# Bilinear form against 128 matrices: weights laid out in 64-row halves, in 19 transfers of uneven size

## The chip, the cores and the metric

One core of a Trainium2 chip. The metric is the device time of one execution in microseconds, the lower the better.

## The reference

For each row b of x and y, and each of 128 weight matrices, one number is computed:

```python
batch, dim_i, dim_j, dim_k = 32, 256, 256, 128
# x: (32, 256), y: (32, 256), weight: (128, 256, 256), all float32
out = np.einsum('bi,bj,kij->bk', x, y, weight)     # (32, 128)
```

The weight is 33.6 MB in fp32 and each of its elements is used for 32 rows of x. x, y and the output are small: 32 KB, 32 KB and 16 KB.

## The kernel before

The sum over i is done on TensorE, with 32 columns of x transposed as the stationary operand and the weight as the moving one; the sum over j, with y, is done on VectorE, which multiplies a row of results by y and adds it up.

At the start x and y come in over the SyncE queue (L51, L54). An identity matrix is made on GpSimd, TensorE transposes x in two pieces (L62), and VectorE casts them to bf16 into `xT` (L67). The piece `ii` holds the rows i = 2p + ii of x on partition p.

The weight comes in 16 tiles of eight k each. A tile (`wtile`, bf16, 128 partitions x 8 x 512) is one transfer, issued by GpSimd (L77), which also casts fp32 to bf16 on the way. A partition p holds the rows 2p and 2p + 1 of each of the eight matrices: 512 consecutive elements, 2 KB of fp32, for each k. There are four buffers, so GpSimd issues the first four transfers at once and then each next one when TensorE has finished with the tile four places ahead.

For each two k of a tile, two matmuls of 512 columns (two k by 256 j) add up the even and the odd rows in one PSUM tile (L82). For each single k VectorE then makes one multiply and add over 256 elements (L93), which leaves one column of `out_sb`. A second short VectorE instruction reads the accumulator out. At the end SyncE stores `out_sb` (L104).

Each engine works through its list in the order in which the loops below are written; the tile framework adds the semaphore waits.

Of the kernel before, what the change touches and what calls it, by code (L numbers as in the profile page):

```python
# [1 line left out]

# [5 lines left out]


@with_exitstack
def kernel(
    ctx: ExitStack,
    tc: tile.TileContext,
    x: bass.AP,
    y: bass.AP,
    weight: bass.AP,
    out: bass.AP,
):
    nc = tc.nc  # L20
    P = 128

    B, I = x.shape
    _, J = y.shape
    K, _, _ = weight.shape
    assert x.shape == (B, I)
    assert y.shape == (B, J)
    assert weight.shape == (K, I, J)
    assert out.shape == (B, K)

    assert I % P == 0
    I_TILES = I // P
    assert K <= P

    K_TILE = 8
    assert K % K_TILE == 0
    NUM_K_TILES = K // K_TILE
    K_SUB = max(1, 512 // J)
    assert K_TILE % K_SUB == 0

    f32 = mybir.dt.float32
    bf16 = mybir.dt.bfloat16

    consts = ctx.enter_context(tc.tile_pool(name="consts", bufs=1))
    wpool = ctx.enter_context(tc.tile_pool(name="wpool", bufs=4))
    psum_pool = ctx.enter_context(tc.tile_pool(name="psum", bufs=6, space=bass.MemoryType.PSUM))
    tpsum_pool = ctx.enter_context(tc.tile_pool(name="tpsum", bufs=2, space=bass.MemoryType.PSUM))
    tmps = ctx.enter_context(tc.tile_pool(name="tmps", bufs=4))

    x_sb = consts.tile([B, I], f32)  # L50
    nc.sync.dma_start(out=x_sb, in_=x)  # L51

    y_sb = consts.tile([B, J], f32)
    nc.sync.dma_start(out=y_sb, in_=y)  # L54

    identB = consts.tile([B, B], f32)
    make_identity(nc, identB)

    xT = consts.tile([P, I_TILES, B], bf16)
    for ii in range(I_TILES):  # L60
        xt_psum = tpsum_pool.tile([P, B], f32)
        nc.tensor.transpose(  # L62
            out=xt_psum,
            in_=x_sb[:, ii::I_TILES],
            identity=identB,
        )
        nc.vector.tensor_copy(out=xT[:, ii, :], in_=xt_psum)  # L67

    out_sb = consts.tile([B, K], f32)

    w_rearr = weight.rearrange("k (i ii) j -> i k (ii j)", ii=I_TILES)

    for kt in range(NUM_K_TILES):
        k0 = kt * K_TILE

        wtile = wpool.tile([P, K_TILE, I_TILES * J], bf16)
        nc.gpsimd.dma_start(out=wtile, in_=w_rearr[:, k0:k0 + K_TILE, :])  # L77

        for ks in range(0, K_TILE, K_SUB):
            psum = psum_pool.tile([P, K_SUB * J], f32)  # L80
            for ii in range(I_TILES):
                nc.tensor.matmul(  # L82
                    out=psum[:B, :].rearrange("b (k j) -> b k j", k=K_SUB),
                    lhsT=xT[:, ii, :],
                    rhs=wtile[:, ks:ks + K_SUB, ii * J:(ii + 1) * J],
                    start=(ii == 0),
                    stop=(ii == I_TILES - 1),
                )

            psum_view = psum[:B, :].rearrange("b (k j) -> b k j", k=K_SUB)  # L90
            for kk in range(K_SUB):
                tmp = tmps.tile([B, J], f32)
                nc.vector.tensor_tensor_reduce(  # L93
                    out=tmp,
                    in0=psum_view[:, kk, :],
                    in1=y_sb,
                    scale=1.0,
                    scalar=0.0,
                    op0=mybir.AluOpType.mult,
                    op1=mybir.AluOpType.add,  # L100
                    accum_out=out_sb[:, k0 + ks + kk:k0 + ks + kk + 1],
                )

    nc.sync.dma_start(out=out, in_=out_sb)  # L104


# [1 line left out]
_INS = ['x', 'y', 'weight']  # L108
_OUTS = [((32, 128), 'float32')]


# [23 lines left out]
```

## Time and profile before

| | us |
|---|---|
| median of 4 runs | 96.57 |
| lowest and highest run | 95.49, 96.80 |
| the profiled execution | 96.36 |
| its span, first to last instruction | 94.5 |
| TensorE matmul busy | 48.3 (51%) |
| VectorE busy | 48.1 (51%) |
| GpSimd busy | 14.6 (15%) |

The time of an execution is a little longer than the span that the profile shows, here by 1.86 us. TensorE and VectorE are each busy for half of the span, and the profile's mean granted clock of TensorE is 0.756 of full speed. The granted clock has two levels, shown as 0.50 (1.2 GHz) and 1.00 (2.4 GHz). DMA rates are counted in bytes written, which for the weight are half of the bytes read.

### The profile page before, as it was taken

What the parts mean: (1) busy time and instruction counts of PE and PEld (TensorE: products, weight loads), DVE (VectorE), ACT (ScalarE), POOL (GpSimd) and SP (SyncE); (2) the same over time, 40 slices, a digit from 0 to 9 for tenths busy, and PEclk for the clock granted to TensorE, in tenths of its full rate; (3) what the DMA queues carried; (4) which work ended last, traced back from release to release, by engine and by line L of the source; (5) the groups of instructions that cost most, each with busy time, mean ns of one, the idle gap of its engine ahead of it and who ended that gap; (6) DMA issues with size and microseconds to landing.
All of it is one profiled execution on the core that took longest, in us unless ns stands there. A gap on an engine that the chain in (4) does not pass through costs nothing.

```text
span 94.5 us, 680 instructions
## 1 busy us (share of the span) xinstructions
PE 48.3 (51%) x130; PEld 15.0 (16%) x130; DVE 48.1 (51%) x258; POOL 14.6 (15%) x22
## 2 busy tenths in 40 slices
PE   0100096775248293937083773935092958761560
PEld 0100031212011130302030211211030303120210
DVE  0100048383919175667456281849275483948290
POOL 5910002012300303030303002032003000000000
PEclk9999999999995555579975555589955555599955
DMA  0699999999999999999999999999999999996000
GB/s 24 67 170 200 147 207 207 208 205 208 207 209 205 208 206 207 208 206 208 207 208 206 208 204 207 206 210 205 208 207 207 208 206 208 206 208 110 3 3 7
DMA packets 16787, 16.88 MB, mean 179 GB/s; under 512 B 304, under 2 KB 16784, under 8 KB 16784
## 3 DMA queue, kind: packets, MB, share of 16 engines
q0 software_dynamic: 16640, 16.78, 108.1%
q1 hardware_dynamic: 144, 0.08, 0.3%
q14 instruction: 3, 0.02, 0.1%
HBM read 33.62 MB, written 0.02 MB: 356 GB/s over the span
## 4 chain that ended last, share of the span: by engine, by line
DMA 78%; PE 9%; issue 6%; POOL 3%; DVE 1%; POOLq 0%; DVEq 0%
DMA wtile<-in_weight_dram 78%; PE psum L82 9%; POOL wtile L77 3%; DVE tmp L93 1%; POOL identB masks.py:199 0%; POOL identB masks.py:197 0%; POOLq masks.py:199 0%; POOLq L130 0%; POOLq L77 0%; POOLq L119 0%; DVE out_sb L93 0%; DVEq L130 0%
## 5 line engine op out<-in xcount | busy, mean ns | idle before, releaser
L82 PE MATMUL psum<-wtile,xT 128*32 128x512 bf16 x128 | 47.9, 541 | 40.4 <-DMA wtile<-in_weight_dram 40.4
L93 DVE CUSTOM_DVE_ANT_0 tmp<-psum,y_sb 32x256 f32<-32x256 f32 x128 | 47.3, 409 | 41.1 <-PE psum L82 38.5
L82 PEld LDWEIGHTS <-xT 128*32 128x32 bf16 x128 | 14.7, 122 | 72.8 <-issue 50.8
L77 POOL DMA_DIRECT2D wtile<-in_weight_dram x16 | 14.1, 886 | 57.6 <-PE psum L82 57.1
L93 DVE DVE_READ_ACCUMULATOR2_ANT out_sb<- 32x1 f32 x128 | 9.1, 71 | 0.0
L67 DVE CAST xT<-xt_psum 128x32 bf16<-128x32 f32 x2 | 0.3, 191 | 3.0 <-PE xt_psum L62 3.0
L62 PE MATMUL xt_psum<-identB,x_sb 32*128 32x32 f32 x2 | 0.4, 312 | 2.7 <-POOL identB masks.py:199 2.7
L62 PEld LDWEIGHTS xt_psum<-identB,x_sb 32*128 32x128 f32 x2 | 0.3, 201 | 2.7 <-POOL identB masks.py:199 2.7
masks.py:199 POOL TENSOR_SCALAR_AFFINE_SELECT identB<-identB 32x32 f32<-32x32 f32 x1 | 0.2, 224 | 0.1
masks.py:197 POOL MEMSET identB<- 32x32 f32 x1 | 0.1, 114 | 0.3 <-POOLq L119 0.3
L119 POOL MEMSET const-float32-0.0<- 128x1 f32 x1 | 0.1, 103 | 0.2 <-issue 0.2
L119 POOL MEMSET const-bfloat16-1.0<- 128x1 bf16 x1 | 0.1, 106 | 0.0
L119 POOL MEMSET const-uint8-127<- 128x1 uint8 x1 | 0.1, 106 | 0.0
L119 POOL MEMSET const-float32-1.0<- 128x1 f32 x1 | 0.1, 103 | 0.0
## 6 DMA issues: line engine op xcount, KB each, us to landing
wtile<-in_weight_dram POOLq DMA_DIRECT2D x16, 1024.0 KB, 16.7
x_sb<-in_x_dram SPq DMA_DIRECT2D x1, 32.0 KB, 1.7
y_sb<-in_y_dram SPq DMA_DIRECT2D x1, 32.0 KB, 1.7
out_dram<-out_sb SPq DMA_DIRECT2D x1, 16.0 KB, 1.4
```

What stands on the lines that cost most here:

```text
L62: nc.tensor.transpose(out=xt_psum, in_=x_sb[:, ii::I_TILES], identity=identB,)
L67: nc.vector.tensor_copy(out=xT[:, ii, :], in_=xt_psum)
L77: nc.gpsimd.dma_start(out=wtile, in_=w_rearr[:, k0:k0 + K_TILE, :])
L82: nc.tensor.matmul(out=psum[:B, :].rearrange("b (k j) -> b k j", k=K_SUB), lhsT=xT[:, ii, :], rhs=wtile[:, ks:ks + K_SUB, ii * J:(ii + 1) ...
L93: nc.vector.tensor_tensor_reduce(out=tmp, in0=psum_view[:, kk, :], in1=y_sb, scale=1.0, scalar=0.0, op0=mybir.AluOpType.mult, op1=mybir.Al ...
L119: nc = _bacc.Bacc("TRN2", target_bir_lowering=False, num_devices=1)
```

## The change

Four things change together.

**Layout of the weight.** A partition now holds four consecutive rows of a matrix (4p to 4p + 3, 1,024 elements, 4 KB of fp32) instead of two. A matrix of 256 rows then fills 64 partitions, and two matrices stand one above the other: the even k of a pair on partitions 0 to 63 (`kg` = 0), the odd k on 64 to 127 (`kg` = 1). A full tile still holds eight k, as 128 x 4 x 1024.

**Matmuls.** For each pair of k there are four steps (`ic`), and in each a matmul of 64 rows and 256 columns for the even k on the upper half and one for the odd k on the lower half, into two PSUM tiles. That makes 512 matmuls of 256 columns in place of 128 of 512. `xT` holds four pieces instead of two, each twice, once per half of the partitions; for that x is loaded twice side by side (`x2_sb`) and four transposes and casts are made.

**Transfers.** The 16 transfers of eight k become 19: one of four k, 14 of eight, then 4, 4, 2 and 2.

**Buffers.** PSUM has four tiles of 256 columns for the results (six of 512 before), and the output scratch `tmp` two buffers instead of four.

```diff
-    K_TILE = 8
-    K_SUB = max(1, 512 // J)
+    CHUNK = 4
+    HALF_P = P // 2
+    K_TILE = 4
+    K_HALF = K_TILE // 2
+    K_SUB = max(1, min(K_HALF, 256 // J))
...
-    psum_pool = ctx.enter_context(tc.tile_pool(name="psum", bufs=6, space=bass.MemoryType.PSUM))
-    tpsum_pool = ctx.enter_context(tc.tile_pool(name="tpsum", bufs=2, space=bass.MemoryType.PSUM))
-    tmps = ctx.enter_context(tc.tile_pool(name="tmps", bufs=4))
+    psum_pool = ctx.enter_context(tc.tile_pool(name="psum", bufs=4, space=bass.MemoryType.PSUM))
+    tmps = ctx.enter_context(tc.tile_pool(name="tmps", bufs=2))
-    x_sb = consts.tile([B, I], f32)
-    nc.sync.dma_start(out=x_sb, in_=x)
+    x2_sb = consts.tile([B, 2, I], f32)
+    nc.sync.dma_start(out=x2_sb[:, 0, :], in_=x)
+    nc.sync.dma_start(out=x2_sb[:, 1, :], in_=x)
+    x2_flat = x2_sb.rearrange("b two i -> b (two i)")
...
-    xT = consts.tile([P, I_TILES, B], bf16)
-    for ii in range(I_TILES):
+    xT = consts.tile([P, CHUNK, B], bf16)
+    for ic in range(CHUNK):
...
-            in_=x_sb[:, ii::I_TILES],
+            in_=x2_flat[:, ic::CHUNK],
...
-    w_rearr = weight.rearrange("k (i ii) j -> i k (ii j)", ii=I_TILES)
-    for kt in range(NUM_K_TILES):
-        k0 = kt * K_TILE
-        wtile = wpool.tile([P, K_TILE, I_TILES * J], bf16)
-        nc.gpsimd.dma_start(out=wtile, in_=w_rearr[:, k0:k0 + K_TILE, :])
-        for ks in range(0, K_TILE, K_SUB):
-            psum = psum_pool.tile([P, K_SUB * J], f32)
-            for ii in range(I_TILES):
-                nc.tensor.matmul(
-                    out=psum[:B, :].rearrange("b (k j) -> b k j", k=K_SUB),
-                    lhsT=xT[:, ii, :],
-                    rhs=wtile[:, ks:ks + K_SUB, ii * J:(ii + 1) * J],
+    w_rearr = weight.rearrange(
+        "(k2 kg) (ip ic) j -> (kg ip) k2 (ic j)", kg=2, ic=CHUNK)
+    sizes = [4] + [8] * 14 + [4, 4, 2, 2]
+    k0 = 0
+    for size in sizes:
+        K_HALF = size // 2
+        wtile = wpool.tile([P, 4, CHUNK * J], bf16)
+        nc.gpsimd.dma_start(
+            out=wtile[:, :K_HALF, :],
+            in_=w_rearr[:, k0 // 2:k0 // 2 + K_HALF, :],
+        )
+        for ks in range(0, K_HALF, K_SUB):
+            psums = []
+            for kg in range(2):
+                psum = psum_pool.tile([P, K_SUB * J], f32)
+                psums.append(psum)
+            for ic in range(CHUNK):
+                for kg in range(2):
+                    p0 = kg * HALF_P
+                    nc.tensor.matmul(
+                        out=psums[kg][:B, :].rearrange(
+                            "b (k j) -> b k j", k=K_SUB
+                        ),
+                        lhsT=xT[p0:p0 + HALF_P, ic, :],
+                        rhs=wtile[p0:p0 + HALF_P, ks:ks + K_SUB,
+                                  ic * J:(ic + 1) * J],
+                        start=(ic == 0),
+                        stop=(ic == CHUNK - 1),
+                    )
...
+                    kdst = k0 + 2 * (ks + kk) + kg
...
-                    accum_out=out_sb[:, k0 + ks + kk:k0 + ks + kk + 1],
+                        accum_out=out_sb[:, kdst:kdst + 1],
```

The order on TensorE, before, around the step from the first weight tile to the second (`wtile_87` and `wtile_117`; numbers tell buffers apart, and what a row waits for stands in brackets):

```order
L82 LDWEIGHTS xT_79
L82 MATMUL psum_110<-wtile_87,xT_79 32x512
L82 LDWEIGHTS xT_79
L82 MATMUL psum_110<-wtile_87,xT_79 32x512
L82 LDWEIGHTS xT_79
L82 MATMUL psum_119<-wtile_117,xT_79 32x512 [waits DMASW1_49]
```

And on TensorE now, at the same step (`wtile_91` is the first tile, of four k, and `wtile_121` the second, of eight):

```order
L99 MATMUL psum_107<-wtile_91,xT_77 32x256
L99 LDWEIGHTS xT_77
L99 MATMUL psum_108<-wtile_91,xT_77 32x256
L99 LDWEIGHTS xT_77 [waits DMASW1_49]
L99 MATMUL psum_123<-wtile_121,xT_77 32x256 [waits DVE_49]
L99 LDWEIGHTS xT_77
L99 MATMUL psum_124<-wtile_121,xT_77 32x256 [waits DVE_49]
L99 LDWEIGHTS xT_77
L99 MATMUL psum_123<-wtile_121,xT_77 32x256
```

Two matmuls of one PSUM tile stood behind each other; now the matmuls of two PSUM tiles alternate, each with a weight load of its own ahead of it, and there are 32 pairs of load and matmul for a full tile in place of eight.

The last weight transfers in GpSimd's list, before:

```order
L77 DMA wtile_447<-in_weight_dram 128x8x512 [waits DMASW0_49,PE_49]
L77 DMA wtile_477<-in_weight_dram 128x8x512 [waits DMASW1_49,PE_49]
L77 DMA wtile_507<-in_weight_dram 128x8x512 [waits DMASW2_49,PE_49]
L77 DMA wtile_537<-in_weight_dram 128x8x512 [waits DMASW3_49,PE_49]
L130 UNCONDITIONAL_BRANCH
```

And now:

```order
L86 DMA wtile_817<-in_weight_dram 128x4x1024 [waits DMASW1_49,PE_49]
L86 DMA wtile_875<-in_weight_dram 128x4x1024 [waits DMASW2_49,PE_49]
L86 DMA wtile_933<-in_weight_dram 128x2x1024 [waits DMASW3_49,PE_49]
L86 DMA wtile_963<-in_weight_dram 128x2x1024 [waits DMASW4_49,PE_49]
L86 DMA wtile_993<-in_weight_dram 128x1024 [waits DMASW5_49,PE_49]
L86 DMA wtile_1009<-in_weight_dram 128x1024 [waits DMASW6_49,PE_49]
```

The last full transfer (`wtile_875`) has four smaller ones behind it, each of which still waits for TensorE (`PE_49`) to leave the buffer four places ahead; the last one takes over the buffer of `wtile_875`.

## Rows read from the trace of the kernel before

**Rows 1.** page, part 2, the span in 40 slices: DMA share in tenths, bytes per time

```profile
DMA  0699999999999999999999999999999999996000
GB/s 24 67 170 200 147 207 207 208 205 208 207 209 205 208 206 207 208 206 208 207 208 206 208 204 207 206 210 205 208 207 207 208 206 208 206 208 110 3 3 7
```

**Rows 2.** page, part 4, the chain that ended last, by engine

```profile
DMA 78%; PE 9%; issue 6%; POOL 3%; DVE 1%; POOLq 0%; DVEq 0%
```

**Rows 3.** waits: engine, line <- releaser: us in total, times, longest

```profile
POOL wtile L77 <- PE psum L82: 57.1, 12, 10.7
...
PE psum L82 <- DMA wtile<-in_weight_dram: 40.4, 16, 8.9
```

**Rows 4.** DMA queues, 12 to 85 us

```profile
DMA packets 14965, 15.11 MB, mean 207 GB/s; under 512 B 224, under 2 KB 14963, under 8 KB 14963
...
q0 software_dynamic: 14963, 15.09, 124.2%
q14 instruction: 2, 0.02, 0.1%
```

**Rows 5.** DMA queues, 27.9 to 28.4 us

```profile
q14 instruction: 1, 0.01, 4.0%
```

**Rows 6.** windows, 3 to 12 us: stretch, its length, engines' busy time, PEclk, DMA share, GB/s

```profile
3.00:4.00 1.00, 0.11 (x1) 0.10 (x1) 0.31 (x2) 1.00 (x2) 1.00 0.84 65
4.00:5.00 1.00, 0.00 (x0) 0.00 (x0) 0.00 (x0) 1.00 (x2) 1.00 0.88 110
...
10.00:11.00 1.00, 0.00 (x0) 0.00 (x0) 0.00 (x0) 0.00 (x0) 1.00 0.95 96
11.00:12.00 1.00, 0.00 (x0) 0.00 (x0) 0.00 (x0) 0.00 (x0) 1.00 1.18 189
```

**Rows 7.** timeline of PE: start us, us, what, count, idle time before it

```profile
12.02 3.57 PE L82 MATMUL psum<-wtile,xT 128*32 128x512 bf16 x8 [8.91 <-DMA wtile<-in_weight_dram]
17.08 3.57 PE L82 MATMUL psum<-wtile,xT 128*32 128x512 bf16 x8 [1.49 <-DMA wtile<-in_weight_dram]
...
83.52 1.89 PE L82 MATMUL psum<-wtile,xT 128*32 128x512 bf16 x8 [1.53 <-DMA wtile<-in_weight_dram]
88.54 2.83 PE L82 MATMUL psum<-wtile,xT 128*32 128x512 bf16 x8 [3.13 <-DMA wtile<-in_weight_dram]
```

**Rows 8.** timeline from 88 us: VectorE and the store

```profile
89.17 0.41 DVE L93 CUSTOM_DVE_ANT_0 tmp<-psum,y_sb 32x256 f32<-32x256 f32 x1 [2.19 <-PE psum L82]
...
91.41 0.41 DVE L93 CUSTOM_DVE_ANT_0 tmp<-psum,y_sb 32x256 f32<-32x256 f32 x1
...
91.76 0.41 DVE L93 CUSTOM_DVE_ANT_0 tmp<-psum,y_sb 32x256 f32<-32x256 f32 x1
...
92.20 0.33 SPq L104 DMA_DIRECT2D out_dram<-out_sb  x1
```

**Rows 9.** timeline of POOL

```profile
1.29 1.01 POOL L77 DMA_DIRECT2D wtile<-in_weight_dram  x1 [0.43 <-issue]
...
15.89 0.88 POOL L77 DMA_DIRECT2D wtile<-in_weight_dram  x1 [10.71 <-PE psum L82]
```

**Rows 10.** page, part 5, weight loads: count, busy, mean ns, idle time before

```profile
L82 PEld LDWEIGHTS <-xT 128*32 128x32 bf16 x128 | 14.7, 122 | 72.8 <-issue 50.8
```

**Rows 11.** windows, 85 to 88 us

```profile
85.00:86.00 1.00, 0.40 (x2) 0.00 (x0) 1.00 (x7) 0.00 (x0) 1.00 1.19 197
86.00:87.00 1.00, 0.00 (x0) 0.00 (x0) 0.98 (x6) 0.00 (x0) 1.00 0.39 64
87.00:88.00 1.00, 0.00 (x0) 0.00 (x0) 0.00 (x0) 0.00 (x0) 1.00 0.08 12
```

**Rows 12.** windows of three stretches, cut where the granted clock changes

```profile
21.10:27.90 6.80, 2.48 (x11) 1.02 (x12) 3.18 (x19) 1.60 (x2) 1.00 1.24 207
27.90:41.50 13.60, 9.59 (x22) 2.65 (x20) 8.86 (x47) 1.95 (x3) 0.50 1.24 207
41.50:48.40 6.90, 2.72 (x12) 1.12 (x13) 3.34 (x19) 1.55 (x2) 0.99 1.25 208
```

More of the change, by code (lines that the diff above doesn't have):

```diff
@@ L29 @@
     assert out.shape == (B, K)
-    assert I % P == 0
-    I_TILES = I // P
+    CHUNK = 4
+    HALF_P = P // 2
+    assert I == HALF_P * CHUNK
     assert K <= P
-    K_TILE = 8
-    assert K % K_TILE == 0
+    assert K % 2 == 0
+    K_TILE = 4
+    assert K % K_TILE == 0 and K_TILE % 2 == 0
+    K_HALF = K_TILE // 2
     NUM_K_TILES = K // K_TILE
-    K_SUB = max(1, 512 // J)
-    assert K_TILE % K_SUB == 0
+    K_SUB = max(1, min(K_HALF, 256 // J))
+    assert K_HALF % K_SUB == 0
     f32 = mybir.dt.float32
@@ L57 @@
     make_identity(nc, identB)
-    xT = consts.tile([P, I_TILES, B], bf16)
-    for ii in range(I_TILES):
-        xt_psum = tpsum_pool.tile([P, B], f32)
+    xT = consts.tile([P, CHUNK, B], bf16)
+    for ic in range(CHUNK):
+        xt_psum = psum_pool.tile([P, B], f32)
         nc.tensor.transpose(
             out=xt_psum,
-            in_=x_sb[:, ii::I_TILES],
+            in_=x2_flat[:, ic::CHUNK],
             identity=identB,
         )
-        nc.vector.tensor_copy(out=xT[:, ii, :], in_=xt_psum)
+        nc.vector.tensor_copy(out=xT[:, ic, :], in_=xt_psum)
@@ L69 @@
     out_sb = consts.tile([B, K], f32)
-    w_rearr = weight.rearrange("k (i ii) j -> i k (ii j)", ii=I_TILES)
-    for kt in range(NUM_K_TILES):
-        k0 = kt * K_TILE
-        wtile = wpool.tile([P, K_TILE, I_TILES * J], bf16)
-        nc.gpsimd.dma_start(out=wtile, in_=w_rearr[:, k0:k0 + K_TILE, :])
-        for ks in range(0, K_TILE, K_SUB):
-            psum = psum_pool.tile([P, K_SUB * J], f32)
-            for ii in range(I_TILES):
-                nc.tensor.matmul(
-                    out=psum[:B, :].rearrange("b (k j) -> b k j", k=K_SUB),
-                    lhsT=xT[:, ii, :],
-                    rhs=wtile[:, ks:ks + K_SUB, ii * J:(ii + 1) * J],
-                    start=(ii == 0),
-                    stop=(ii == I_TILES - 1),
-                )
[L90 to L100, printed above, removed]
-                    accum_out=out_sb[:, k0 + ks + kk:k0 + ks + kk + 1],
-                )
@@ new lines @@
+    w_rearr = weight.rearrange(
+        "(k2 kg) (ip ic) j -> (kg ip) k2 (ic j)", kg=2, ic=CHUNK)
+    sizes = [4] + [8] * 14 + [4, 4, 2, 2]
+    assert sum(sizes) == K
+    k0 = 0
[24 more added lines that the diff above has]
+                    )
+            for kg in range(2):
+                psum_view = psums[kg][:B, :].rearrange(
+                    "b (k j) -> b k j", k=K_SUB
+                )
+                for kk in range(K_SUB):
+                    kdst = k0 + 2 * (ks + kk) + kg
+                    tmp = tmps.tile([B, J], f32)
+                    nc.vector.tensor_tensor_reduce(
+                        out=tmp,
+                        in0=psum_view[:, kk, :],
+                        in1=y_sb,
+                        scale=1.0,
+                        scalar=0.0,
+                        op0=mybir.AluOpType.mult,
+                        op1=mybir.AluOpType.add,
+                        accum_out=out_sb[:, kdst:kdst + 1],
+                    )
+        k0 += size
```

## The prediction

> **What bounds the kernel now.** I read the two lines of the 40 slices first [rows 1]: the DMA engines are at 9 tenths from the third slice to the thirty-sixth, and what they write runs at about 207 GB/s throughout. The chain says the same: 78% of the span is DMA and only 9% TensorE [rows 2]. The waits show that nobody holds the DMA engines up. GpSimd sits 57.1 us waiting for TensorE before it issues the next weight transfer [rows 3], which looks like a bottleneck, but TensorE itself waits 40.4 us for weights; the GpSimd wait only means that four tiles are always queued. So time is a sum of three pieces: how the DMA stream starts, how long the 16 MB take, and what follows when the last bytes land.
>
> The stream: between 12 and 85 us it writes 15.11 MB [rows 4], which over 16 engines is 12,937 bytes per us and engine, or 1,024 bytes (one packet, 2,048 bytes of fp32 read) each 79.2 ns. A tile is 64 packets per engine, 5.07 us, and TensorE's bursts stand that far apart [rows 7]. Start: from 3 to 12 us the rate is below 207 [rows 6]. End: TensorE begins the last tile at 88.54 [rows 7], VectorE begins its last reduction at 91.76 and needs 0.41 more, the store goes out at 92.20 [rows 8], and 2.3 us later the span of 94.5 ends. The execution took 96.36 us, 1.86 more than its span; the median of the runs is 96.57, and with 4 runs between 95.49 and 96.80 about 1% is what a measurement can tell from no change.
>
> **Part 1: half as many packets, twice as long.** The new layout gives a partition four consecutive rows of the weight: a packet reads 4 KB and writes 2 KB; each engine has 512 of them instead of 1,024. What one costs is not in the trace, so it is bounded. If time goes by bytes alone, nothing is gained: 0 is one end. For the other, compare a weight packet with a larger one. Weight packets occupy 124.2% of 16 engines in 73 us, 14,963 of them: 97 ns each [rows 4], 98 without the 224 tiny completion writes. An instruction fetch, one of the two packets of 8 KB in that stretch (0.02 MB together, and not counted under 8 KB), takes 4.0% of 16 engines in 0.5 us, 320 ns [rows 5]. The slope is (320 - 98)/(8,192 - 2,048) = 36 ps per byte, so 2,048 more bytes add 74 ns where a second packet adds 79.2: 5 ns saved, times 512 = 2.6 us. The rounding of the 4.0% makes it 1.9 to 3.3. I take **-2.0**, the low side, because a packet's time is its latency and not its pitch. A tile of eight then takes about 4.94 us.
>
> **Part 2: smaller transfers at the end.** Now the last tile holds eight outputs, and 3.63 us pass from its first matmul (88.54) to VectorE's end (91.76 + 0.41 = 92.17). Afterwards it holds two: eight matmuls of 256 columns on two row halves. The stretch at granted clock 0.50 (1.2 GHz) has 22 matmuls in 9.59 us, 0.436 us for 512 columns; at 1.00 (2.4 GHz) 11 take 2.48 us, 0.225 [rows 12]. So a 256-column matmul is 0.22 or 0.11 us. If the two halves run side by side, four pairs at 0.22 take 0.88; VectorE starts about 0.2 later (89.17 against 88.54 plus two matmuls) and needs 0.35 + 0.41 for two reductions (91.41 to 91.76, and the last one's own time). Together 1.84 us: **-1.8**. At full clock it is -2.2, with the halves in turn at 1.2 GHz -0.9.
>
> **Part 3: the issue behind it.** Four buffers remain, so the last transfer (tile 18 of 0 to 18) waits in GpSimd's queue until TensorE is done with tile 14, the last one of eight. TensorE needs 16 pairs, 3.6 us; GpSimd follows 0.3 later (12.02 + 3.57 to 15.89 [rows 7, 9]); and the first weight bytes moved about 1.8 us after the first issue began (1.29 [rows 9], against the 3 to 4 us stretch [rows 6]): 5.7 us. Meanwhile tiles 15 to 17, ten outputs, keep the DMA engines busy 10/8 x 4.94 = 6.2 us. It just fits: **0**. Nothing else stands behind that wait, since GpSimd has only weight issues left.
>
> By the Trainium skill ("DMA: Bandwidth & Descriptors", Anatomy of one DMA) a transfer costs about 2.0 us plus its bytes, which speaks against cutting transfers: three more would make the sum 6 us worse. The trace disagrees as long as a queue is filled: 207 GB/s holds across all tile boundaries [rows 1].
>
> **Part 4: more instructions.** TensorE's pairs of weight load and matmul grow from 128 to 512. Two instruction fetches fell into the 73 us [rows 4], each 0.32 us of one DMA engine [rows 5]. Scaled by those pairs it would be eight, six more. The engines don't finish together: from 85 to 88 us the rate falls 197, 64, 12 [rows 11], and the last of them sets the landing. Ends: 0 if all hit engines with slack, 6 x 0.32 = 1.9 if all hit the slowest. I take two: **+0.6**.
>
> **At nothing.** The second copy of x, two more transposes and casts, and y behind one more issue lie ahead of the first matmul, where TensorE idles 8.91 us [rows 7]. Without that cover they would cost half a microsecond. VectorE's 128 reductions stay: 0.35 pitch x 8 = 2.8 us per tile, under 4.94; with only two pairs of PSUM buffers it is still TensorE's 0.88 per pair or VectorE's 0.70 that sets the pace. Three more issues on GpSimd lie in its 57 us of waiting. The first tile is half as large and TensorE starts earlier, but the DMA stream doesn't care. What may move is the stream's ramp: 65 GB/s in the fourth microsecond, 110 in the next, 96 from 10 to 11 [rows 6], in all 2.2 us of transfer lost over the nine rows from 3 to 12 us, against 207. If the loss goes by packets, half of it (1.1) is saved; it could as well grow by that. I take 0.
>
> **Sum:** 96.36 - 2.0 - 1.8 + 0 + 0.6 = 93.2 us.
>
> **Rivals.**
> 1. *The halves run one after the other at 1.2 GHz* (the slower side). Then TensorE needs 512 x 0.22 = 113 us. From the first landing near 9.5 (12.02 less half a tile) that ends at 122.5, and with 0.2 + 0.76 + 2.3 and 1.86 the time is 128. It decides once a matmul takes over 4.94/32 = 0.154 us on average. At 2.4 GHz even serial matmuls take 0.11 and fit. The stretch at 0.50, with TensorE busy 9.59 of 13.6 us, is followed by one at 0.99 [rows 12], and a serial TensorE would at 0.50 be busy without a break, so staying low is unlikely: 4%. The milder form, serial with a changing clock, 6%: tile 14 takes up to 7 us, tile 18 is issued 3.4 us later, arrives 3 us late, and part 2 gives back 0.9: about 97.
> 2. *Weight loads no longer hide.* A load takes 0.122 us [rows 10]. If each had to wait for the matmul on its own half, a pair would be 0.34 and a tile 5.4 us at 1.2 GHz: TensorE bound, about 101. It decides at a pair of 0.31 us. Against it: now every load is on the same rows as the matmul ahead of it, and 22 matmuls still take 0.436 each where 512 columns at 1.2 GHz are 0.427 [rows 12]. 3%. The Trainium skill ("TensorE: Matmul & The Clock Gate", Part 3) has this rule: loads overlap matmuls in flight only on other row groups. This trace shows otherwise.
> 3. *Packets cost by their bytes alone*, or are cut to the old size: part 1 gives 0, 95.2 us. For it: the rate is flat and the engines look full. 14%.
> 4. *The ramp shrinks with the packets*: 92.1, to 91.3 with the full clock at the end. 12%.
> 5. *The last transfers come late*: part 3's margin is 0.5 us; if tile 18 goes into an empty queue it pays the 1.8 us of a fresh issue, 95 us; two such, 96.8; one for each added transfer, 98.6. 7%, of which 1% for the last. That last case is what the skill's rule under part 3 comes to here.
>
> **How the numbers follow.** Forecast 54%, between 92.3 and 94.6 by the ends of parts 2 and 4. The range has to take in the lighter ramp, the packets without gain and most late tails: **91.3 to 96.0**, leaving out mainly the cases of rivals 1 and 2. Faster by over 1% (under 95.6): forecast, rival 4, two thirds of rival 3, half of rival 5, 0.79. Within 1%: the rest of rival 3, some of 5, a little of the mild serial case, 0.11. Slower: rivals 1 and 2 and what is left, 0.10.
>
> **What would show it.** Right: about 8,200 weight packets instead of 16,384, a steady rate of 211 to 213 GB/s, bursts of TensorE 4.94 us apart, TensorE's busy time not over 60 us, about 1.9 us from the last burst's start to VectorE's end, and eight or so instruction fetches. Wrong: the packet count unchanged or the rate still 207 (part 1); matmuls starting 0.2 us apart in turn with GpSimd's issues late (rival 1); a gap in DMA share ahead of the last transfer (rival 5). The largest risk is whether two 64-row halves share the array, which no row here can show.

## The result, and the profile after

The changed kernel takes 90.61 us (median of 11 runs, 90.29 to 91.03). The kernel before, timed beside it, takes 96.11 (16 runs). The ratio is 0.943, with a 95% interval of 0.940 to 0.946. The forecast was 93.2 with a range of 91.3 to 96.0: the sign is right, the gain is 5.5 us where 3.2 was forecast, and the time lies under the range.

The profiled execution took 91.03 us against 96.36, its span 89.3 against 94.5. The page of the changed kernel, parts 1 and 2 (the span, and in 40 slices the DMA share and the rate written):

```profile
span 89.3 us, 1511 instructions
...
DMA  0799999999999999999999999999999999998600
GB/s 19 113 206 215 211 213 212 209 214 209 216 212 213 208 212 213 211 213 210 216 208 212 212 213 214 208 217 207 212 215 210 214 208 212 214 210 155 115 2 7
```

The DMA engines are still at 9 tenths nearly throughout, so the stream of weights (the transfers that fill `wtile`, one behind the other) bounds the kernel as before. Against [rows 1] three things are to be seen: the rate is 212 instead of 207 in the middle, it is full from the third slice on, with no 147 in the fifth, and the end falls off in steps (155, 115).

The page, part 3 (queue, kind: packets, MB, share of 16 engines):

```profile
q0 software_dynamic: 8496, 16.78, 100.6%
...
q8 instruction: 4, 0.07, 0.3%
q14 instruction: 3, 0.02, 0.1%
```

8,192 weight packets in place of 16,384 (the rest of the 8,496 are completion writes). Instruction fetches are seven, four of them of 16 KB. The steady stream of the changed kernel, DMA queues from 30 to 70 us:

```profile
DMA packets 4254, 8.49 MB, mean 212 GB/s; under 512 B 128, under 2 KB 128, under 8 KB 4251
...
q0 software_dynamic: 4251, 8.44, 112.0%
```

4,251 less 128 small ones are 4,123 weight packets in 40 us on 16 engines: 155.2 ns for 4 KB of reads, where two packets of 2 KB took 158.4 [rows 4].

The start, in windows of one microsecond (PEclk, DMA share and GB/s are the last three columns):

```profile
3.00:4.00 1.00, 0.66 (x4) 0.62 (x5) 0.55 (x4) 1.00 (x3) 1.00 0.81 89
4.00:5.00 1.00, 0.00 (x0) 0.00 (x0) 0.00 (x0) 0.60 (x1) 1.00 1.18 217
...
10.00:11.00 1.00, 0.00 (x0) 0.00 (x0) 0.00 (x0) 0.00 (x0) 1.00 1.12 211
```

The first row is nearly as slow as before (89 for 65), but the second has 217 instead of 110, and from 10 to 11 us there is 211 instead of 96 [rows 6]. TensorE's timeline shows what that is worth, and what comes last:

```profile
6.79 1.89 PE L99 MATMUL psum<-wtile,xT 64*32 64x256 bf16 x16 [3.13 <-DMA wtile<-in_weight_dram]
11.79 3.75 PE L99 MATMUL psum<-wtile,xT 64*32 64x256 bf16 x32 [3.12 <-DMA wtile<-in_weight_dram]
...
21.73 2.75 PE L99 MATMUL psum<-wtile,xT 64*32 64x256 bf16 x32 [1.26 <-DMA wtile<-in_weight_dram]
28.01 3.75 PE L99 MATMUL psum<-wtile,xT 64*32 64x256 bf16 x32 [3.53 <-DMA wtile<-in_weight_dram]
...
77.30 4.79 PE L99 MATMUL psum<-wtile,xT 64*32 64x256 bf16 x48 [2.19 <-DMA wtile<-in_weight_dram]
...
85.56 0.61 PE L99 MATMUL psum<-wtile,xT 64*32 64x256 bf16 x8 [0.95 <-DMA wtile<-in_weight_dram]
```

With these rows and [rows 7] the difference splits into five pieces; the third is what the others leave over. A tile's burst begins when the slowest of the 16 DMA engines has landed its part. In the kernel before, the second burst (17.08) has 16 k behind it, at 8 x 79.2 ns = 0.634 us each: the stream started 6.94 us late against a steady one. In the changed kernel the second burst (11.79) has 12 k behind it, at 4 x 155.2 = 0.621 each: 4.34. This **start offset** is used below.

| piece | before | after | difference | forecast |
|---|---|---|---|---|
| start offset | 6.94 | 4.34 | -2.60 | 0 |
| 128 k at the steady rate | 81.10 | 79.46 | -1.64 | -2.0 |
| lost between second and last burst | 0.50 | 1.76 | +1.26 | +0.6 |
| last burst to VectorE's end | 3.63 | 1.41 | -2.22 | -1.8 |
| from there to the end of the span | 2.3 | 2.3 | 0 | 0 |
| span | 94.5 | 89.3 | -5.2 | -3.2 |

The row "last burst to VectorE's end" is read from VectorE's last reduction and the store:

```profile
86.56 0.41 DVE L117 CUSTOM_DVE_ANT_0 tmp<-psum,y_sb 32x256 f32<-32x256 f32 x1
...
87.00 0.33 SPq L129 DMA_DIRECT2D out_dram<-out_sb  x1
```

86.56 + 0.41 less 85.56 is 1.41.

The start offset follows the slowest engine. What all 16 engines together lost at the start is smaller. DMA queues from 0 to 20 us, first the kernel before and then the changed one:

```profile
q0 software_dynamic: 3028, 3.07, 98.9%
```

```profile
q0 software_dynamic: 1745, 3.48, 94.6%
```

At the weights' steady rates (15.09 MB in 73 us [rows 4], and 8.44 MB in 40 us; 0.01 MB is 0.05 us) these bytes are 14.85 and 16.49 us of transfer, so 5.15 and 3.51 us of the first 20 are lost: the start gave **1.6 us**, and the other 1.0 of the 2.60 is how far the slowest engine was behind the rest.

That part didn't last. From the burst at 21.73 to the one at 28.01 us pass 6.28 us where a tile needs 4.97, while all engines together keep their rate (209, 216, 212 and 213 GB/s in slices 10 to 13 above): one or some of them fell behind there, and it is counted in the third row. The rest of that row lies at the end: from 77.30 to 85.56 us pass 8.26 us for twelve k that need 7.45, 0.8 too many, where the kernel before lost nothing (5.02 us for its last tile).

So the span's -5.2 is -1.64 at the start, -1.64 by the rate, +0.81 behind 77.30 us and -2.22 after the last burst; the -0.5 that is left is a smaller distance of the slowest engine from the rest.

### The profile page after: what moved, and what is told of

The parts are those of the page before. It is cut to its first block, busy times and chain, and to the rows that moved or that the text cites. A ratio compares the mean times of both kernels' runs of the same rounds, so it can differ in the third digit from the quotient of the medians.

```text
span 89.3 us, 1511 instructions
## 1 busy us (share of the span) xinstructions
PE 52.7 (59%) x516; PEld 34.1 (38%) x516; DVE 48.4 (54%) x260; POOL 14.2 (16%) x25
## 3 DMA queue, kind: packets, MB, share of 16 engines
q0 software_dynamic: 8496, 16.78, 100.6%
## 4 chain that ended last, share of the span: by engine, by line
DMA 75%; PE 13%; issue 6%; POOL 2%; DVE 0%; DVEq 0%; POOLq 0%
DMA wtile<-in_weight_dram 75%; PE psum L99 13%; POOL wtile L86 2%; DVE tmp L117 0%; POOL identB masks.py:199 0%; DVEq L155 0%; POOL identB masks.py:197 0%; POOLq masks.py:199 0%; POOLq L155 0%; POOLq L86 0%; POOLq L144 0%; DVE out_sb L117 0%
## 5 line engine op out<-in xcount | busy, mean ns | idle before, releaser
L99 PE MATMUL psum<-wtile,xT 64*32 64x256 bf16 x512 | 52.0, 357 | 30.5 <-DMA wtile<-in_weight_dram 28.7
L99 PEld LDWEIGHTS <-xT 64*32 64x32 bf16 x512 | 33.5, 117 | 48.9 <-DMA wtile<-in_weight_dram 33.0
```

What stands on the lines that cost most here:

```text
L99: nc.tensor.matmul(out=psums[kg][:B, :].rearrange("b (k j) -> b k j", k=K_SUB), lhsT=xT[p0:p0 + HALF_P, ic, :], rhs=wtile[p0:p0 + HALF_P, ...
```

## The experiments

Two theories stood against each other for the start. **P**: what is lost there is lost per packet, so long packets alone shorten it. **F**: the smaller first transfer does it. A third, **A**, lays it to the addresses that the first packets read. Twelve kernels were run; the time of the kernel before, beside them, was 95.74, 96.50 and 96.28 us in three groups, the second of them on another chip; between groups the ratios are compared.

**Layout alone.** Changed kernel with equal transfers:

```diff
-    sizes = [4] + [8] * 14 + [4, 4, 2, 2]
+    sizes = [8] * 16
```

> The changed kernel with 16 equal transfers of eight k. Theory P (long packets themselves make the stream's start shorter, because what is lost there is lost per packet): the start stays short, all engines past the first two tiles within about 1 us of each other, no fall of the rate from 10 to 11 us; only the end is given back (3.4 us instead of 1.4 from the last matmul's start to VectorE's end) less the gap ahead of the last small transfer (0.6): about 92.0 us. Theory F (the short start comes from the first transfer being half as large): the start loses 2.3 us more: about 94.4 us, and the rate falls again between the first two tiles.

Measured: 93.70 us (4 runs, 93.58 to 93.77), ratio 0.977 (0.971 to 0.983). Its second burst:

```profile
15.57 3.33 PE L99 MATMUL psum<-wtile,xT 64*32 64x256 bf16 x32 [1.80 <-DMA wtile<-in_weight_dram]
```

The start offset is 15.57 - 16 x 0.621 = 5.64: under the 6.94 of before and over the 4.34 of the change. From 9 to 11 us, where the second transfer begins, the rate was 168 and 180 GB/s, a milder fall than F foresaw. The time lies between the two theories' 92.0 and 94.4. Neither alone is right.

**Sizes alone.** The kernel before with the 19 transfers:

```diff
-    for kt in range(NUM_K_TILES):
-        k0 = kt * K_TILE
+    k0 = 0
+    for size in [4] + [8] * 14 + [4, 4, 2, 2]:
...
+        k0 += size
```

> The kernel before with the 19 transfers of 4, 14 x 8, 4, 4, 2, 2. Theory P: the stream keeps 207 GB/s and its slow start, and only the end is shorter, by about 1.8 us less a gap ahead of the last transfer: about 94.4 us. Theory F: the start is shorter too, by 2.3 us: about 92.1 us.

Measured: 93.06 us (92.73 to 93.55), ratio 0.971 (0.964 to 0.978), again between the theories. Its second burst has 12 k behind it:

```profile
12.99 3.57 PE L83 MATMUL psum<-wtile,xT 128*32 128x512 bf16 x8 [3.95 <-DMA wtile<-in_weight_dram]
```

12.99 - 12 x 0.634 is an offset of 5.39. So going from eight k to four in the first transfer is worth about 1.5 us with short packets (6.94 to 5.39) and 1.3 with long ones (5.64 to 4.34); and long packets are worth 1.3 with a first transfer of eight and about 1.0 with four. These offsets are of the slowest engine in single executions. The bytes of all engines from 0 to 20 us, layout alone and then sizes alone, give smaller and steadier figures:

```profile
q0 software_dynamic: 1666, 3.32, 93.0%
```

```profile
q0 software_dynamic: 3184, 3.21, 99.8%
```

Counted as above, 4.27 and 4.47 us are lost, between the 5.15 of before and the 3.51 of the change. Long packets are worth 0.9 to 1.0 us and the sizes 0.7 to 0.8, whichever comes first, and together they make the 1.6. With sizes alone the rate still fell from 6 to 9 us (169, 157 and 150 GB/s).

**Short packets in the new layout.** Two transfers for a tile, each with half of a partition's row:

```diff
-            out=wtile[:, :K_HALF, :],
-            in_=w_rearr[:, k0 // 2:k0 // 2 + K_HALF, :],
...
+        for h in range(2):
...
+                out=wtile[:, h, :K_HALF, :],
+                in_=w_rearr[:, k0 // 2:k0 // 2 + K_HALF,
+                            h * 2 * J:(h + 1) * 2 * J],
...
```

> The changed kernel with each transfer cut into two, one for rows 0 and 1 of each four and one for rows 2 and 3, so that a packet again reads 2 KB and writes 1 KB; layout, matmuls and the order of tiles stay. Theory P: the steady rate falls to 207 GB/s (+1.8 us) and the slow start comes back (+2.3): about 94.7 us. Theory A (the start depends on which addresses the first packets read, not on their number): +1.8 alone, about 92.4 us. If time goes by bytes alone, the rate stays at 212 and the time at 90.6.

Measured: 95.06 us (93.75 to 95.79), ratio 0.982 (0.972 to 0.993): on both sides of P's 94.7 and above A's 92.4 in every run. DMA queues, 30 to 70 us:

```profile
DMA packets 8278, 8.26 MB, mean 206 GB/s; under 512 B 251, under 2 KB 8275, under 8 KB 8275
```

206 GB/s with the layout and matmuls of the change: the steady rate goes with the length of a packet. Its tile with k 4 to 11 was complete for TensorE at 13.20 us, an offset of 5.60 by the short packets' rate, like the 5.39 of the short packets above. The runs spread over 2 us, and there are twice as many transfers, which may cost at the start as well, so the rate is the firm part of this run.

**Longer packets still.** Eight rows of a matrix on a partition, four matrices on quarters of 32 partitions, packets that read 8 KB:

```diff
-    CHUNK = 4
-    HALF_P = P // 2
+    CHUNK = 8
+    G = 4
+    HALF_P = P // G
...
-    sizes = [4] + [8] * 14 + [4, 4, 2, 2]
+    sizes = [4] + [8] * 14 + [4, 4, 4]
...
```

The loops over the two halves now run over four quarters; with it x is loaded four times, PSUM has eight tiles, and a full tile has matmuls of 512 columns.

> Eight rows of a matrix on a partition, four matrices on quarters of 32 partitions: packets read 8 KB and write 4 KB, 4,096 of them. Transfers are 4, 14 x 8, 4, 4, 4. If each packet carries a fixed cost of about 4 ns beside its bytes, the steady rate rises from 212 to 215 GB/s (4.88 us per tile of eight), and the stream is 1.0 us shorter; the last transfer of four gives back about 1.9 us at the end: 91 to 92 us. If 4 KB packets already run at the rate of the bytes, or 8 KB ones are cut in two, the rate stays at 212.

Measured: 90.62 us (90.28 to 91.57), the time of the change. DMA queues, 30 to 70 us:

```profile
DMA packets 2220, 8.56 MB, mean 214 GB/s; under 512 B 137, under 2 KB 137, under 8 KB 2217
...
q0 software_dynamic: 2217, 8.52, 105.9%
```

214 GB/s: 2,217 less 137 are 2,080 packets, 307.7 ns each, where two of 4 KB take 310.4. Doubling the packet saves 3.2 ns per pair from 2 to 4 KB and 2.7 from 4 to 8 KB. That fits a fixed piece of some 3 ns in every packet, beside about 76 ns for 2 KB of reads. The forecast of 215 was near; the time came out better than its 91 to 92.

**Six weight buffers.**

```diff
-    wpool = ctx.enter_context(tc.tile_pool(name="wpool", bufs=4))
+    wpool = ctx.enter_context(tc.tile_pool(name="wpool", bufs=6))
```

> The changed kernel with six weight buffers instead of four. If the fall of the rate from 81 to 83 us is the last transfer waiting for TensorE to leave its buffer, GpSimd issues it some 10 us earlier, the fall disappears, and the time is 0.5 to 1.0 us lower, about 89.9. If the fall is only the engines finishing apart, nothing changes (90.6).

Measured: 90.46 us (90.32 to 90.62), ratio 0.943 (0.936 to 0.950): not told apart from the change. But the windows show that the fall was that wait. The changed kernel from 80 us:

```profile
80.00:81.00 1.00, 1.00 (x13) 0.78 (x10) 0.91 (x7) 0.08 (x1) 0.50 1.12 209
81.00:82.00 1.00, 1.00 (x13) 0.58 (x8) 0.91 (x5) 0.46 (x1) 0.65 0.82 158
82.00:83.00 1.00, 0.53 (x9) 0.41 (x10) 0.79 (x6) 0.00 (x0) 1.00 0.81 135
83.00:84.00 1.00, 0.85 (x13) 0.38 (x8) 0.80 (x5) 0.00 (x0) 1.00 0.92 152
...
85.00:86.00 1.00, 0.44 (x8) 0.30 (x8) 0.34 (x2) 0.00 (x0) 1.00 0.01 2
```

Its last transfer was issued in that stretch, behind a wait for TensorE of 4.96 us:

```profile
75.42 0.54 POOL L86 DMA_DIRECT2D wtile<-in_weight_dram  x1 [2.84 <-PE psum L99]
80.92 0.54 POOL L86 DMA_DIRECT2D wtile<-in_weight_dram  x1 [4.96 <-PE psum L99]
```

With six buffers the same stretch, from 81 us:

```profile
81.00:82.00 1.00, 1.00 (x13) 0.81 (x9) 0.91 (x6) 0.00 (x0) 0.50 1.09 203
82.00:83.00 1.00, 1.00 (x14) 0.77 (x11) 0.82 (x7) 0.00 (x0) 0.50 1.11 213
83.00:84.00 1.00, 1.00 (x15) 0.78 (x13) 1.00 (x5) 0.00 (x0) 0.77 0.35 66
```

203 and 213 in place of 158 and 135. What then comes last is TensorE, in one burst without a break, at granted clock 0.50 until past 83 us, with VectorE's reductions close behind it. The last transfer's first weight load comes at 85.11, 7.48 us behind the burst's start, as the steady rate has it (7.45), but the median hardly moved:

```profile
77.63 8.20 PE L99 MATMUL psum<-wtile,xT 64*32 64x256 bf16 x80 [1.69 <-DMA wtile<-in_weight_dram]
...
85.11 0.43 PEld L99 LDWEIGHTS <-xT 64*32 64x32 bf16 x8 [0.26 <-DMA wtile<-in_weight_dram]
```

This run's own second burst came at 13.20 us (offset 5.75), although its first transfers are those of the change: in one execution the slowest engine can be over 1 us later than in another. Three other kernels with the first transfers of the change (halves in turn, 512 columns, and 512 columns with six buffers) had 11.84, 11.68 and 11.70. Over all engines there is hardly a difference, with 3.44 MB from 0 to 20 us:

```profile
q0 software_dynamic: 1730, 3.44, 94.4%
```

3.70 us lost, against 3.51 in the change, and the execution took 90.62 us against 91.03. So the offset of one execution doesn't say what the start costs in time, and the theories of the start are judged by all engines' bytes and by the medians.

**First transfer of eight, six and two, with six buffers.** Three kernels differ from the one above in one line, with the end kept as near as the sum of 128 allows (each has one or two small transfers fewer there):

```diff
-    sizes = [4] + [8] * 14 + [4, 4, 2, 2]
+    sizes = [8] * 15 + [4, 2, 2]          # eight
+    sizes = [6] + [8] * 14 + [4, 4, 2]    # six
+    sizes = [2] + [8] * 15 + [4, 2]       # two
```

> The changed kernel with six weight buffers, the first transfer of eight k in place of four (15 x 8, then 4, 2, 2); to be set beside the run with six buffers and the sizes of the change (90.5 us). The end has the same two last transfers, so what differs is the start. Theory F (the smaller first transfer is half of the shorter start): the rate falls where the second transfer begins, and the time is 1.0 to 1.5 us more, about 91.7. Theory P (long packets alone): within 0.3 of 90.5.

> Six buffers and the first transfer of six k (6, 14 x 8, 4, 4, 2); the same start otherwise. Theory F1 (what is lost at the start grows with the size of the first transfer): between the runs with four (90.5 us) and eight (91.8), about 91.1. Theory F2 (four is special, and any other first transfer brings the fall of the rate where the next one begins): 91.5 to 92.

> Six buffers and the first transfer of two k (2, 15 x 8, 4, 2). Theory F1: below the run with four, 90.0 to 90.3. Theory F2: the rate falls where the second transfer begins, 91 to 92.

Measured medians: two 92.98, four 90.46, six 90.74, eight 91.81 us (ratios 0.965, 0.943, 0.943, 0.954). From four to eight the median grows by 1.35 us, or 1.1 by the ratios, whose intervals just touch (0.936 to 0.950 and 0.947 to 0.961); that is what F says. But it is not the smaller the better: six is not told apart from four, and two is the worst of all, so F1 falls, and so does F2 with six. The windows of the kernel with eight, where its second transfer begins:

```profile
8.00:9.00 1.00, 0.00 (x0) 0.00 (x0) 0.00 (x0) 0.00 (x0) 1.00 1.08 203
9.00:10.00 1.00, 0.03 (x2) 0.03 (x3) 0.00 (x0) 0.00 (x0) 1.00 1.16 186
10.00:11.00 1.00, 1.00 (x11) 0.78 (x12) 0.00 (x0) 0.00 (x0) 1.00 1.07 197
```

186 and 197, about 0.2 us of transfer against the 212 GB/s of the middle. More is missing earlier: from 3 to 6 us this kernel has 58, 160 and 195 GB/s, the one with a first transfer of four and the same six buffers 84, 201 and 207. All engines' bytes from 0 to 20 us in the kernel with eight:

```profile
q0 software_dynamic: 1679, 3.34, 94.3%
```

That is 4.17 us lost, 0.5 more than the 3.70 with four; the rest of the 1.1 to 1.35 is not shown to lie at the start. The second bursts of eight and of six:

```profile
15.45 3.33 PE L99 MATMUL psum<-wtile,xT 64*32 64x256 bf16 x32 [1.93 <-DMA wtile<-in_weight_dram]
```

```profile
13.27 3.74 PE L99 MATMUL psum<-wtile,xT 64*32 64x256 bf16 x32 [2.29 <-DMA wtile<-in_weight_dram]
```

The offsets are 5.52 and 4.58. The profile of the kernel with two is of an execution over 1 us longer than its others and isn't read here.

**Two transfers of two first.** Again with six buffers:

```diff
-    sizes = [4] + [8] * 14 + [4, 4, 2, 2]
+    sizes = [2, 2] + [8] * 14 + [4, 4, 2, 2]
```

> Six buffers, and the first transfer of four k cut into two of two. If the slow part of the start is the beginning of the first two transfers and small ones pass it sooner, the time falls a little more, by up to 0.5 us, to about 90.0. If the size of the second transfer matters for nothing, 90.5. If every transfer at the start costs on its own, 91 or more.

Measured: 91.43 us (91.11 to 91.81), 1.0 more than with one transfer of four. The third case came nearest. All engines' bytes from 0 to 20 us:

```profile
q0 software_dynamic: 1681, 3.31, 93.5%
```

4.31 us are lost, 0.6 more than with one transfer of four, although the same addresses are read in packets of the same length. So addresses alone don't set what the start loses.

**Halves in turn.** The loops exchanged, four matmuls on one half and then four on the other:

```diff
-            for ic in range(CHUNK):
-                for kg in range(2):
+            for kg in range(2):
+                for ic in range(CHUNK):
```

> The changed kernel with the loops over ic and kg exchanged: four matmuls on the upper 64 rows, then four on the lower, so that neighbours in the list are on the same rows. Theory S (the halves run side by side in the changed kernel): a full tile of 32 matmuls takes 6.8 us at granted clock 0.50 instead of 3.75, TensorE is then busy without a break, the clock goes up more of the time, and it ends 1 to 3 us later, 91.5 to 93.5. If the halves already run one after the other, nothing changes (90.6).

Measured: 90.54 us (90.45 to 90.80), no change. By the expectation that would mean that the halves run one after the other, but the traces say the opposite. First the changed kernel (two full tiles, one at each clock), then this one at 0.50:

```profile
28.00:31.70 3.70, 3.69 (x32) 2.42 (x32) 2.36 (x13) 0.00 (x0) 0.50 1.12 211
42.20:45.00 2.80, 2.52 (x32) 1.59 (x32) 2.10 (x13) 0.00 (x0) 1.00 1.12 211
```

```profile
67.20:70.80 3.60, 3.60 (x32) 2.49 (x32) 2.36 (x13) 0.00 (x0) 0.50 1.13 213
```

32 matmuls of 256 columns in 3.69 us at 0.50 are 0.115 each, and 0.113 in turn; one by one, half of the 0.436 us for 512 columns [rows 12] would be 0.218. And they start in pairs: in the changed kernel at 28.198 and 28.204 us, then 28.411 and 28.417; in turn at 67.295 and 67.309, then 67.509 and 67.522. So two run at a time in both kernels.

Whether TensorE's list had the order of the loops in this run is not on record. In the run with short packets it did not work in that order, where the loops ask, for each pair of k, for four matmuls on the first of a tile's two transfers and then four on the second:

```profile
6.02 1.04 PE L101 MATMUL psum<-wtile,xT 64*32 64x256 bf16 x8 [2.42 <-DMA wtile<-in_weight_dram]
8.08 1.03 PE L101 MATMUL psum<-wtile,xT 64*32 64x256 bf16 x8 [1.02 <-DMA wtile<-in_weight_dram]
```

Eight ran before the wait for the second transfer, so the order of the loops is not always the engine's order. The experiment didn't do what it was meant for, and what serial halves would cost was not measured.

**Matmuls of 512 columns.**

```diff
         K_HALF = size // 2
+        K_SUB = min(K_HALF, 512 // J)
```

> The changed kernel with matmuls of 512 columns (two pairs of k at once) where a transfer holds at least four k: 264 pairs of load and matmul instead of 512. Theory I (instruction fetches of 16 KB hold up one DMA engine each, and the slowest engine sets the landing): two of the four fetches go, the time falls by 0.3 to 0.6 us to about 90.2. If the fetches fall on engines with slack, 90.6.

Measured: 90.57 us (90.44 to 90.99), the time of the change. The page, part 3, and TensorE's last burst:

```profile
q8 instruction: 2, 0.03, 0.1%
```

```profile
82.02 4.01 PE L100 MATMUL psum<-wtile,xT 64*32 64x512 bf16 x24 [1.34 <-DVE out_sb L118]
```

Two of the 16 KB fetches are gone, as foreseen, but the last burst waited for VectorE to leave a PSUM tile and then ran for 4.01 us. What fewer fetches are worth is not settled by it.

**512 columns, six buffers, eight PSUM banks.**

```diff
-    wpool = ctx.enter_context(tc.tile_pool(name="wpool", bufs=4))
-    psum_pool = ctx.enter_context(tc.tile_pool(name="psum", bufs=4, space=bass.MemoryType.PSUM))
+    wpool = ctx.enter_context(tc.tile_pool(name="wpool", bufs=6))
+    psum_pool = ctx.enter_context(tc.tile_pool(name="psum", bufs=8, space=bass.MemoryType.PSUM))
...
+        K_SUB = min(K_HALF, 512 // J)
...
```

> The changed kernel with six weight buffers, matmuls of 512 columns and eight PSUM banks for results (the transposes share them). If the tail of the run with 512 columns was held up by TensorE waiting for VectorE to leave a PSUM tile, that wait is gone, and the stream's gain of two fetches and of the earlier last issue comes through: 89.5 to 89.9 us. If the end is set otherwise, 90.5.

Measured: 90.47 us (90.02 to 91.58), ratio 0.938 (0.934 to 0.942) against 0.943 (0.940 to 0.946) of the change. The intervals overlap; the 89.5 to 89.9 that were expected weren't reached. No version was shown to beat the change.

## Why the prediction was right or wrong

- **What bounds the kernel** was right: the stream of weights, and the time as start, transfer and end. But the rate was read as 207 GB/s throughout and across all tile boundaries, where [rows 1] has 147 in the fifth slice, behind the first transfer.
- **Part 1** was right in kind and a little high: -1.64 for -2.0. The fixed piece of a packet was bounded from one instruction fetch and came out at 5 ns, taken as 4; three packet lengths put it near 3, 1.6 us over 512 packets.
- **Part 2** was right; the last burst fell into a stretch at 2.4 GHz (85 to 86 us had granted clock 1.00 in that execution), so the end named for the full clock, -2.2, applied.
- **Part 3** was wrong in its margin. 6.2 us of queued transfers were counted from the slowest engine's landing of tile 14 (77.30 us), which would have lasted to 83.5; the engines ahead of it ran out sooner, the rate fell to 158, 135 and 152 from 81 us on, behind the issue at 80.92, and 0.8 us were lost where 0 was forecast.
- **Part 4** had the fetches nearly right in number (seven for eight, but four of them twice as large). The +0.6 did not show: the slowest engine's distance, in which it would lie, went down by about 0.5. What the fetches cost by themselves is not separated.
- **"At nothing"** is the step that failed: "What may move is the stream's ramp ... I take 0", and "The first tile is half as large ... but the DMA stream doesn't care". Over all engines the start gave 1.6 us, of 5.2 in the span; in the forecast's own nine rows from 3 to 12 us, the transfer lost fell from 2.2 to 0.6 us. Long packets bring 0.9 to 1.0 of it and the sizes of the transfers 0.7 to 0.8. The ends of plus or minus 1.1 took in either of the two effects and not their sum.
- The other misses nearly cancel: +0.4 in part 1, -0.4 in part 2, +0.8 in part 3 and -1.1 at the slowest engine (-0.5 for +0.6). So the 2.0 us by which the span came out shorter than forecast look like the start alone, and that is luck.
- **Rivals 1 and 2** did not come: 32 matmuls of a tile take 3.69 us at 1.2 GHz, load and all. Rival 3 did not come: the rate rose. Rival 4 was right by its mechanism, with 1.1 for 0.9 to 1.0, but it left out the sizes. Rival 5 came in part and small. The 2.0 us for each transfer that the Trainium skill gives ("DMA: Bandwidth & Descriptors", Anatomy of one DMA) did not show as time: with three transfers more, 212 GB/s holds across the boundaries of the middle.
- Two bounds don't follow from their own terms: with the ends of parts 2 and 4 the forecast goes from 92.2 to 95.4, not from 92.3 to 94.6, and rival 4 with the full clock comes to 91.7, not 91.3.

What stays open: why packets of twice the length lose less at the start, why with long packets a first transfer of eight k loses more than one of four or six, and why two is worse again.

## What to carry to other kernels

A kernel that streams its data has a start as well as a rate: take what all engines have moved by a time well behind it, compare that with the steady rate, and see whether a change can touch what is missing, before it is booked at nothing. The moment at which one tile is complete shows the slowest engine alone. Where the transfers bound the time, longer contiguous packets still pay at 2 to 8 KB, by a few nanoseconds each. Small last transfers shorten the end; here their wait for a buffer took back 0.8 of the 2.2 us, and six buffers brought the last bytes in time and still didn't move the median, with TensorE and VectorE then last. A range for an unknown term should take in the sum of the effects that act on it.

## What the runs showed of the hardware

- A weight packet that reads 2, 4 or 8 KB takes 79.2, 155.2 and 307.7 ns of one engine in the steady stream: this fits about 3 ns fixed in each.
- Matmuls on the two row halves run two at a time, at 0.115 us each for 256 columns at 1.2 GHz; their starts come in pairs some 6 to 14 ns apart. At granted clock 1.00 a full tile took 2.52 us of TensorE (0.079 each).
- With packets of the same length, first transfers of two, four, six and eight k went with 92.98, 90.46, 90.74 and 91.81 us; the ends differ by one or two small transfers.
- The slowest of the 16 DMA engines can be over 1 us later in one execution than in another with the same first transfers (second tile complete at 11.68 to 11.84 us in three kernels, at 13.20 in a fourth), while all engines together have moved nearly the same (3.44 to 3.47 MB by 20 us).
- Instruction fetches came in pieces of 8 KB and, with 512 pairs of load and matmul, four more of 16 KB, counted among the same 16 DMA engines.
